# First-half v, k and q projections of a hybrid encoder layer at 512 columns, with their weights in borrowed rings

## The chip, the core and the metric

The kernel runs on one core of a Trainium2 chip. TensorE (PE) multiplies; its weight loads are shown as an engine of their own (PEld). VectorE (DVE), ScalarE (ACT) and GpSimd (POOL) do the rest, and SyncE (SP) issues every DMA of this kernel. The metric is the device time of one execution in microseconds, as a median of several executions.

## The reference

One layer of an encoder. Two inputs of width 1024, a prompt of 2048 tokens and a sample of 64 tokens, go through an RMS norm and one wide input projection; its columns feed a differential attention, a retention and their gates; two output projections, a merge and a last projection follow.

```python
def layer_inputs(x, norm_g, w_in, b_gate, qn_g, kn_g):
    h = rmsnorm(x, norm_g) @ w_in
    qa, ka, va, za, qb, kb, vb, zb, ga, gb = jnp.split(h, _split_points(), axis=-1)
    qa = rmsnorm(qa.reshape(B, T, H_A, 2, DK_A), qn_g)
    ka = rmsnorm(ka.reshape(B, T, H_A, 2, DK_A), kn_g)
    va = va.reshape(B, T, H_A, DV_A)
    ...

def layer_output(x, oa, ob, za, zb, ga, gb, subln_g, lam_init, w_oa, w_ob, w_out):
    oa = (rmsnorm(oa, subln_g) * (1.0 - lam_init)).reshape(B, T, W_A) * jax.nn.silu(za)
    ob = rmsnorm(ob).reshape(B, T, W_B) * jax.nn.silu(zb)
    m = ga * (oa @ w_oa) + gb * (ob @ w_ob)
    return x + m @ w_out
```

`qa`, `ka` and `va` (here q, k and v of the attention) have 512 columns each, four heads of 128. The normed k and v are outputs as well. Everything is float32.

## The kernel before

Every large product is made of three: both operands are split into a high part, rounded to the matmul's faster float32 form, and a low part, the difference; high x high, high x low and low x high are summed in PSUM.

The program is written by a planner in Python. Tasks are generators with priorities; a loop (line 80) runs the first task that is ready by estimated clocks of the engines (`P`, `A`, `V`, `G`, `ld`, lines 113 to 132), and what it emits fixes the order of instructions on TensorE, ACT and DVE. Buffers are rings counted by `take` and `give` (lines 97 to 111), with the sizes of `BUFS` (line 33). So each of these three engines runs its queue in a fixed order, and an instruction that waits holds all behind it.

The projections (`w_stream`, line 1442) go through the tokens in two halves of 1024; the sample belongs to the first. For each half they go through `w_in` in blocks of 256 columns.

- x: `x_prep` (line 247) loads tiles of 128 tokens, `x_norm` (272) norms them (sum of squares on ACT, line 277; small steps, lines 280 to 289; times the norm's weight `gn` on DVE, line 294). `gn` is a row of 1024 numbers, loaded into all 128 partitions by one DMA. `x_tile` (298) transposes a tile by TensorE (line 308, eight transposes) and splits it into `xh` and `xl` (lines 315, 316).
- W: `w_load` (332) loads a block of 256 columns in four pieces of 256 rows (two K blocks each, 256 KB) into the ring `ws` of 3; `w_split` (344) casts a piece to `wh` on ACT (line 354) and takes the difference `wl` on POOL (line 361; two of the first pieces on DVE, line 358) into the ring `w` of 12 tiles, which is six pieces.
- `mm_group` (374) issues the 24 products of one output: 8 K blocks x 3. `natural` (392) uses the x tile as weights and W as the moving operand, 256 columns wide; two x tiles share one PSUM bank and one evacuation. `transposed` (542) uses W as weights and moves up to 512 tokens.
- v is evacuated by `fin_va` (495), k and q by `fin_qk` (417; norm per head, four transposes, split, stores into DRAM scratch `kT`, `qT`). Their outputs pass through rings `ev` (3), `tlo` (2) and `thi` (1).

The first half's order is v (two blocks), k (two), q first block, mark `kqv0`, q second block, mark `kqv1`, then the retention's projections and the gates. `z_stream` (1497) starts the attention of heads 0 and 1 at `kqv0` of a half and that of heads 2 and 3 at `kqv1`; it loads k, v and q again from DRAM scratch through the rings `K` (4), `V` (4) and `q` (2), and `ath` and `atl` (2 each) hold split probabilities. Its tasks have a higher priority than projections, which fill TensorE otherwise. When both streams are done, the last stage makes the output projections (lines 1339 to 1341 and 1404 to 1406).

Ahead of everything stand 16 products of `ones` (line 1555) without use for the result.

## Time and profile before

| | us |
|---|---|
| median of 3 runs | 2037.01 (2036.58 to 2038.7) |
| the profiled execution | 2037.63 |
| its span, first to last instruction | 2035.9 |
| TensorE / ACT / DVE / POOL busy | 1999.1 / 962.7 / 985.9 / 420.5 |
| products at line 384, 256 columns, x as weights (3 groups) | 289, 283 and 283 ns each, 1024 in each group |
| products at line 384, 512 columns, W as weights (3 groups) | 397, 391 and 391 ns each, 768 in each group |

In the profile a line names the source line, the engine, the operation, the tile written and the tiles read, with shapes; the number in square brackets is how long the engine sat idle before it, and what ended that. The order "mm<-wh,xh" gives the moving operand first and the weights second. Products overlap: a product's own time is longer than the step from one start to the next, and the step is what counts for throughput. fp32 products, such as those of `ones`, stand as two records each.

### The profile page before, as it was taken

What the parts mean: (1) busy time and instruction counts of PE and PEld (TensorE: products, weight loads), DVE (VectorE), ACT (ScalarE), POOL (GpSimd) and SP (SyncE); (2) the same over time, 40 slices, a digit from 0 to 9 for tenths busy, and PEclk for the clock granted to TensorE, in tenths of its full rate; (3) what the DMA queues carried; (4) which work ended last, traced back from release to release, by engine and by line L of the source; (5) the groups of instructions that cost most, each with busy time, mean ns of one, the idle gap of its engine ahead of it and who ended that gap; (6) DMA issues with size and microseconds to landing.
All of it is one profiled execution on the core that took longest, in us unless ns stands there. A gap on an engine that the chain in (4) does not pass through costs nothing. (4 is left out here: it accounts for less than half of the span.)

```text
span 2035.9 us, 35819 instructions
## 1 busy us (share of the span) xinstructions
PE 1999.1 (98%) x13058; PEld 1826.1 (90%) x13058; DVE 985.9 (48%) x2671; ACT 962.7 (47%) x2123; POOL 420.5 (21%) x394
## 2 busy tenths in 40 slices
PE   7999999999999999999999999999999979999999
PEld 7999999999998999999999888888888868888997
DVE  6265765643331210546856545635653365444442
ACT  5334766644343332535766655634654453333321
POOL 1222112121012221221211212122131343222210
PEclk9999999999999999999999999999999989999999
DMA  6663545345565463563352252463233665454531
GB/s 217 202 195 115 162 138 145 101 124 156 151 170 133 130 194 93 152 200 127 113 155 91 84 154 75 115 188 99 63 100 113 187 200 154 144 150 136 148 101 58
DMA packets 332160, 281.57 MB, mean 138 GB/s; under 512 B 65104, under 2 KB 307408, under 8 KB 331984
## 3 DMA queue, kind: packets, MB, share of 16 engines
q1 hardware_dynamic: 331984, 279.29, 46.8%
q8 instruction: 103, 1.69, 0.4%
q14 instruction: 73, 0.60, 0.1%
HBM read 187.71 MB, written 91.49 MB: 137 GB/s over the span
## 5 line engine op out<-in xcount | busy, mean ns | idle before, releaser
L384 PE MATMUL mm<-xh,wh 128*128 128x512 f32 (+2 forms) x1280 | 459.8, 359 | 0.0
L384 PE MATMUL mm<-xh,wl 128*128 128x512 f32 (+2 forms) x1280 | 452.0, 353 | 0.0
L384 PE MATMUL mm<-xl,wh 128*128 128x512 f32 (+2 forms) x1280 | 451.7, 353 | 0.0
L361 POOL TENSOR_TENSOR wl<-ws,wh 128x512 fp32r<-128x512 f32 x190 | 252.1, 1342 | 832.5 <-ACT wh L354 643.5
L384 PE MATMUL mm<-wh,xh 128*128 128x256 f32 x1088 | 313.3, 288 | 0.5 <-ACT xh L315 0.3
L384 PE MATMUL mm<-wl,xh 128*128 128x256 f32 x1088 | 307.7, 283 | 0.7 <-DVE wl L358 0.3
L384 PE MATMUL mm<-wh,xl 128*128 128x256 f32 x1088 | 307.7, 283 | 0.2 <-DVE xl L316 0.2
L384 PEld LDWEIGHTS mm<-xh,wl 128*128 128x128 f32 x1280 | 241.0, 188 | 31.1
L384 PEld LDWEIGHTS mm<-xh,wh 128*128 128x128 f32 x1280 | 241.3, 189 | 30.6 <-issue 0.2
L384 PEld LDWEIGHTS mm<-xl,wh 128*128 128x128 f32 x1280 | 241.4, 189 | 30.0
L384 PEld LDWEIGHTS mm<-wh,xh 128*128 128x128 f32 x1088 | 204.8, 188 | 3.3 <-ACT xh L315 0.5
L384 PEld LDWEIGHTS mm<-wl,xh 128*128 128x128 f32 x1088 | 204.9, 188 | 3.0 <-DVE wl L358 0.5
L384 PEld LDWEIGHTS mm<-wh,xl 128*128 128x128 f32 x1088 | 204.7, 188 | 0.4 <-DVE xl L316 0.4
L569 ACT COPY ev<-mm 128x512 f32<-128x512 f32 x140 | 71.6, 512 | 213.4 <-PE mm L384 200.4
L865 DVE TENSOR_TENSOR atl<-at,ath 128x512 fp32r<-128x512 f32 (+1 forms) x144 | 93.6, 660 | 151.6 <-ACT ath L863 151.6
L782 ACT ACTIVATE row<-row,a_mx 128x1024 f32<-128x1024 f32 (+7 forms) x160 | 153.5, 963 | 24.2 <-DVE a_mx L762 24.0
L752 DVE CUSTOM_DVE_ANT_0 row<-s,dfar 128x512 f32<-128x512 f32 (+2 forms) x192 | 117.3, 631 | 72.4 <-PE s L744 71.3
L354 ACT CAST wh<-ws 128x512 fp32r<-128x512 f32 x192 | 117.0, 619 | 65.4 <-PE mm L384 37.5
L863 ACT CAST ath<-at 128x512 fp32r<-128x512 f32 (+1 forms) x144 | 79.6, 563 | 99.1 <-PE at L850 98.6
L743 PE MATMUL s<-K,q 128*128 128x512 f32 (+3 forms) x320 | 120.3, 381 | 3.0 <-DVE a_acc L752 2.8
L803 DVE SCALAR_TENSOR_TENSOR row<-row,a_w 128x1024 f32<-128x1024 f32 (+4 forms) x96 | 101.4, 1064 | 40.5 <-ACT row L800 40.2
L744 PE MATMUL s<-K,q 128*128 128x512 f32 (+3 forms) x320 | 115.7, 363 | 0.0
(196 smaller groups left out, 3922.1 us busy)
## 6 DMA issues: line engine op xcount, KB each, us to landing
ws<-in_w_in_dram SPq DMA_DIRECT2D x192, 256.0 KB, 3.0
q<-qT SPq DMA_DIRECT2D x128, 128.0 KB, 3.0
V<-vN SPq DMA_DIRECT2D x24, 512.0 KB, 5.4
K<-kT SPq DMA_DIRECT2D x48, 256.0 KB, 4.2
gt<-gaT SPq DMA_DIRECT2D x64, 132.0 KB, 2.1
gt<-gbT SPq DMA_DIRECT2D x64, 132.0 KB, 2.1
xt<-in_x_prompt_dram SPq DMA_DIRECT2D x16, 512.0 KB, 5.0
kn<-in_cache_k_T_dram SPq DMA_DIRECT2D x32, 256.0 KB, 3.2
```

The costliest lines, as they stand in the source:

```text
L354: nc.scalar.copy(h, st)
L361: nc.gpsimd.tensor_sub(l, st, h.bitcast(F32))
L384: nc.tensor.matmul(ps, p, q, start=c == 0 and i == 0, stop=c == KC - 1 and i == 2)
L569: nc.scalar.copy(ev, ps)
L743: nc.tensor.matmul(ps, q1s, kk, start=True, stop=False)
L744: nc.tensor.matmul(ps, q2s, kk, start=False, stop=True)
L752: nc.vector.tensor_tensor_reduce(out=units[k0 // 1024][:, k0 % 1024:k0 % 1024 + n], in0=ps, in1=tab, scale=-SLOPES[h], scalar=3.0e38, op0= ...
L782: nc.scalar.activation(u, u, AF.Exp, bias=mx, scale=-1.0, accum_out=lp[:, k:k + 1])
L803: nc.vector.scalar_tensor_tensor(out=u0, in0=u0, scalar=w[:, 0:1], in1=u1, op0=ALU.mult, op1=ALU.add)
L863: nc.scalar.copy(ah[:, :w], at[:, :w])
L865: nc.vector.tensor_sub(al[:, :w], at[:, :w], ah[:, :w].bitcast(F32))
```

## The change

In the first half v, k and q become one block of 512 columns each, in that order, and both marks come behind q. `natural` then takes one x tile to a PSUM bank (24 products of 512 columns, not 48 of 256). W comes in eight pieces of 128 rows x 512 columns for a block, each still 256 KB. Their split parts go into rings that are free at that time: v's and q's into the attention's `K` and `V` (as [128, 2, 512], two K blocks in a tile), k's first six K blocks into `w` and its last two into `q`. The first eight pieces are staged in `ws`, `ath` and `atl` together (`STAGE`). Odd pieces of these blocks have their difference on DVE. A W unit is now one K block throughout, and a ring's tile is given back when its last K block is used.

The weight row of the norm is loaded for the first half as a single row into a cleared tile `gz`; two products with `ones` (1/128 everywhere) spread it over the partitions, and DVE copies the result times 128 into `gn`. The warm-up has 12 products, not 16. The second x tile is loaded after four W pieces, the third after eight.

k, q and v are evacuated and stored one x tile at a time with all four heads (`nh=4`): `kT` and `qT` in runs of 128 tokens, `vN` and the outputs in rows of 512 columns. The second half is as before.

```diff
+STAGE = ["ws", "ws", "ws", "ath", "ath", "atl", "atl", "ws"]
...
-            yield lambda: self.xfly < XFLY and (half > 0 or self.wloads >= min(2 * j, 4))
+            yield lambda: self.xfly < XFLY and (half > 0 or self.wloads >= min(4 * j, 8))
...
-            if j == 0:
+            if j == 0 and half == 0:
+                tg = self.ld(self.gz[0:1, :], self.i["norm_g"][0:1, :], 4096)
+                self.ld(self.ident, self.i["c_ident"], 1 << 16)
+                for k in range(2):
+                    sl = slice(512 * k, 512 * k + 512)
+                    ps = self.psum("s")
+                    nc.tensor.matmul(ps, self.ones, self.gz[:, sl], start=True, stop=True)
+                    t = self.P(2048)
+                    nc.vector.tensor_scalar_mul(gn[:, sl], ps, 128.0)
+                    tg = self.V(512, t)
+                self.give("row", tg)
+            elif j == 0:
                 tg = self.ld(gn, self.i["norm_g"][0].partition_broadcast(128), 1 << 19)
-                if half == 0:
-                    self.ld(self.ident, self.i["c_ident"], 1 << 16)
...
-            for c0 in self.order[half]:
-                for q in range(4):
-                    yield from self.take("ws")
-                    st = self.sb(self.wp, [128, 2, 256], "ws")
+            for c0, wide in self.order[half]:
+                for q in range(8 if wide else 4):
+                    tag = STAGE[q] if self.wloads < 8 else "ws"
+                    yield from self.take(tag)
+                    pool = self.wp if tag == "ws" else self.ap
+                    if wide:
+                        st = self.sb(pool, [128, 512], tag, "ws")
+                        src = self.i["w_in"][0, 128 * q:128 * q + 128, c0:c0 + 512]
...
+    def w_room(self, wide, nw, q):
+
+        if not wide:
+            tags, pool, shape = ("w", "w"), self.wp, [128, 2, 256]
+        elif nw != 1:
+            tags, pool, shape = ("K", "V"), self.ap, [128, 2, 512]
+        elif q < 6:
+            tags, pool, shape = ("w", "w"), self.wp, [128, 1, 512]
+        else:
+            tags, pool, shape = ("q", "q"), self.ap, [128, 2, 512]
+        u = q % 2 if shape[1:] == [2, 512] else 0
+        if u == 0:
+            for tag in tags:
+                yield from self.take(tag)
+            self.wroom = [self.sb(pool, shape, tag, n, F32R) for tag, n in zip(tags, ("wh", "wl"))]
+        if not wide:
+            return self.wroom, tags
+        return [w[:, u] for w in self.wroom], tags if u == shape[1] - 1 else ()
...
-            if n in (0, 2):
-                yield t
-                nc.vector.tensor_sub(l, st, h.bitcast(F32))
-                t = self.V(512, t)
...
+                if wide and q % 2:
+                    yield t
+                    nc.vector.tensor_sub(l, st, h.bitcast(F32))
+                    t = self.V(512, t)
...
-    def natural(self, half, fin, fresh=False):
+    def natural(self, half, fin, fresh=False, wide=False):
         us = []
         tiles = self.xtiles(half)
-        for j0 in range(0, len(tiles), 2):
-            pair = tiles[j0:j0 + 2]
+        per, n = (1, 512) if wide else (2, 256)
+        for j0 in range(0, len(tiles), per):
+            group = tiles[j0:j0 + per]
...
-                self.give(tag, self.st(d[2 * g:2 * g + 2, :, t0:t0 + rt].rearrange("h p t -> p h t"),
-                                       s.bitcast(F32).rearrange("p (h t) -> p h t", h=2), nu << 17))
+                self.give(tag, self.st(d[hs, :, t0:t0 + rt].rearrange("h p t -> p h t"),
+                                       s.bitcast(F32).rearrange("p (h t) -> p h t", h=nh), nh * nu << 16))
...
-        first = ORD(fva0, fva, fk, fq, m0, m1)
+        wva = (va, lambda half: self.natural(half, self.fin_va(0, 4), True, True), True)
+        wk = (ka, lambda half: self.natural(half, self.fin_qk("k", 0, 4), False, True), True)
+        wq = (qa, lambda half: self.natural(half, self.fin_qk("q", 0, 4), False, True), True)
+        first = ([wva, wk, wq, m0, m1], ORD(fva0, fva, fk, fq, m0, m1))
...
+            self.res["row"].free.pop()
+            self.gz = self.row("gz")
+            nc.gpsimd.memset(self.gz, 0.0)
             warm = self.psum("at")
-            for _ in range(16):
+            for _ in range(12):
```

More of the change, by code (lines that the diff above doesn't have):

```diff
@@ L172, in consts @@
         self.ld(self.rzeta, i["c_rzeta"])
-        self.qinv = c("qinv", [128, 2, 8])
+        self.qinv = c("qinv", [128, 3, 8])
         for h in range(4):
@@ L177, in consts @@
                                  (SLOPES[h] / 0.125) ** 2 / 64.0)
+            nc.vector.memset(self.qinv[:, 2, 2 * h:2 * h + 2], (SLOPES[h] / 0.125) ** 2 / 64.0)
         self.gq = c("gq", [128, 1])
@@ L333, in w_load @@
         for half in range(2):
-            for c0 in self.order[half]:
-                for q in range(4):
-                    yield from self.take("ws")
-                    st = self.sb(self.wp, [128, 2, 256], "ws")
-                    t = self.ld(st, self.i["w_in"][0, 256 * q:256 * q + 256, c0:c0 + 256]
-                                .rearrange("(c p) n -> p c n", p=128), 1 << 18)
-                    self.wst.append((st, t))
+            for c0, wide in self.order[half]:
[7 more added lines that the diff above has]
+                    else:
+                        st = self.sb(pool, [128, 2, 256], tag)
+                        src = self.i["w_in"][0, 256 * q:256 * q + 256, c0:c0 + 256] \
+                            .rearrange("(c p) n -> p c n", p=128)
+                    t = self.ld(st, src, 1 << 18)
+                    self.wst.append((st, t, tag))
@@ L341, in w_load @@
                     self.wloads += 1
                     yield self.pe
+    def w_room(self, wide, nw, q):
[5 more added lines that the diff above has]
+            tags, pool, shape = ("w", "w"), self.wp, [128, 1, 512]
+        else:
+            tags, pool, shape = ("q", "q"), self.ap, [128, 2, 512]
[7 more added lines that the diff above has]
+        return [w[:, u] for w in self.wroom], tags if u == shape[1] - 1 else ()
@@ L344, in w_split @@
     def w_split(self):
         nc = self.nc
-        for n in range(4 * (len(self.order[0]) + len(self.order[1]))):
-            yield lambda: len(self.wst) > 0
-            st, t = self.wst.pop(0)
-            yield from self.take("w", 2)
-            if t > self.pe:
-                yield t
-            h = self.sb(self.wp, [128, 2, 256], "w", "wh", F32R)
-            l = self.sb(self.wp, [128, 2, 256], "w", "wl", F32R)
-            nc.scalar.copy(h, st)
-            t = self.A(512, self.pe)
-            if n in (0, 2):
-                yield t
-                nc.vector.tensor_sub(l, st, h.bitcast(F32))
-                t = self.V(512, t)
-            else:
-                nc.gpsimd.tensor_sub(l, st, h.bitcast(F32))
-                t = self.G(512, t)
-            self.give("ws", t)
-            self.wq.append((h, l, t))
+        nw = n = 0
@@ new lines, in w_split @@
+        for c0, wide in self.order[0] + self.order[1]:
+            for q in range(8 if wide else 4):
+                yield lambda: len(self.wst) > 0
+                st, t, tag = self.wst.pop(0)
+                (h, l), tags = yield from self.w_room(wide, nw, q)
+                if t > self.pe:
+                    yield t
+                nc.scalar.copy(h, st)
+                t = self.A(512, self.pe)
+                if wide and q % 2:
+                    yield t
+                    nc.vector.tensor_sub(l, st, h.bitcast(F32))
+                    t = self.V(512, t)
+                else:
+                    nc.gpsimd.tensor_sub(l, st, h.bitcast(F32))
+                    t = self.G(512, t)
+                self.give(tag, t)
+                if wide:
+                    self.wq.append((h, l, t, tags))
+                else:
+                    self.wq.append((h[:, 0], l[:, 0], t, ()))
+                    self.wq.append((h[:, 1], l[:, 1], t, tags))
+                n += 1
+            nw += wide
@@ L366, in w_unit @@
     def w_unit(self, us, c):
-        if len(us) <= c // 2:
+        if len(us) <= c:
             yield lambda: len(self.wq) > 0
             us.append(self.wq.pop(0))
-        u = us[c // 2]
+        u = us[c]
         if u[2] > self.pe:
             yield u[2]
-        return u[0][:, c % 2], u[1][:, c % 2]
+        return u
     def mm_group(self, ps, n, us, wsl, x, wfirst, last):
@@ L378, in mm_group @@
         for c in range(KC):
-            a, b = yield from self.w_unit(us, c)
+            a, b, _, tags = yield from self.w_unit(us, c)
             a, b = a[:, wsl], b[:, wsl]
@@ L385, in mm_group @@
                 self.P(n)
-            if c % 2:
-                if last:
-                    self.give("w", self.pe + LAT, 2)
-                if c < KC - 1:
-                    yield self.pe
-    def natural(self, half, fin, fresh=False):
+            if last:
+                for tag in tags:
+                    self.give(tag, self.pe + LAT)
+            if c % 2 and c < KC - 1:
+                yield self.pe
+    def natural(self, half, fin, fresh=False, wide=False):
         us = []
         tiles = self.xtiles(half)
-        for j0 in range(0, len(tiles), 2):
-            pair = tiles[j0:j0 + 2]
+        per, n = (1, 512) if wide else (2, 256)
+        for j0 in range(0, len(tiles), per):
+            group = tiles[j0:j0 + per]
             yield from self.take("mm")
             ps = self.psum("mm")
-            for u, (src, r, seg, col) in enumerate(pair):
+            for u, (src, r, seg, col) in enumerate(group):
                 if fresh:
@@ L402, in natural @@
                     yield self.xt_ready[j0 + u]
-                yield from self.mm_group(ps[:r, 256 * u:256 * u + 256], 256, us, slice(0, 256),
+                yield from self.mm_group(ps[:r, n * u:n * u + n], n, us, slice(0, n),
                                          (seg, slice(col, col + r)), False, j0 + u == len(tiles) - 1)
-                if u < len(pair) - 1:
+                if u < len(group) - 1:
                     yield self.pe
             t0 = 1024 * half + 128 * j0 if j0 < 8 else T
-            self.spawn(fin(ps[:r, :256 * len(pair)], r, len(pair), t0, self.pe + LAT), 0, "w")
+            self.spawn(fin(ps[:r, :n * len(group)], r, len(group), t0, self.pe + LAT), 0, "w")
             yield self.pe
@@ L415, in rows_out, with fin_qk @@
                        nu * nbytes)
-    def fin_qk(self, which, g):
+    def fin_qk(self, which, g, nh=2):
         nc = self.nc
         ep = self.ep
+        hs = slice(2 * g, 2 * g + nh)
         def fin(ps, r, nu, t0, t):
-            n, ng, rt = 256 * nu, 4 * nu, r * nu
+            n, ng, rt = 128 * nh * nu, 2 * nh * nu, r * nu
             yield from self.take("ev")
@@ L445, in fin @@
                 nc.vector.scalar_tensor_tensor(out=ms, in0=ms, scalar=64.0 * EPS,
-                                               in1=self.qinv[:r, g, :ng], op0=ALU.add, op1=ALU.mult)
+                                               in1=self.qinv[:r, 2 if nh == 4 else g, :ng], op0=ALU.add, op1=ALU.mult)
             else:
@@ L457, in fin @@
                 if t0 < T:
-                    dst = self.o["k_prompt"][0, 0, t0:t0 + rt, 2 * g:2 * g + 2]
+                    dst = self.o["k_prompt"][0, 0, t0:t0 + rt, hs]
                 else:
-                    dst = self.o["k_sample"][0, 0, :, 2 * g:2 * g + 2]
-                ts = self.rows_out(dst.rearrange("t h c d -> t (h c d)"), raw, nu, 1 << 17)
+                    dst = self.o["k_sample"][0, 0, :, hs]
+                ts = self.rows_out(dst.rearrange("t h c d -> t (h c d)"), raw, nu, nh << 16)
             yield from self.take("tp")
@@ L464, in fin @@
             for u in range(nu):
-                for h in range(2):
-                    nc.tensor.transpose(tp[:, h * rt + u * r:h * rt + u * r + r],
-                                        raw[:, u * 256 + h * 128:u * 256 + h * 128 + 128],
+                for h in range(nh):
+                    c = 128 * (nh * u + h)
+                    nc.tensor.transpose(tp[:, h * rt + u * r:h * rt + u * r + r], raw[:, c:c + 128],
                                         self.ident[:r, :r])
@@ L472, in fin @@
             yield from self.take("tlo")
-            hi = self.sb(ep, [128, 512], "thi", dt=F32R)[:, :2 * rt]
-            lo = self.sb(ep, [128, 512], "tlo", dt=F32R)[:, :2 * rt]
-            pt = tp[:, :2 * rt]
+            hi = self.sb(ep, [128, 512], "thi", dt=F32R)[:, :nh * rt]
+            lo = self.sb(ep, [128, 512], "tlo", dt=F32R)[:, :nh * rt]
+            pt = tp[:, :nh * rt]
             if which == "q":
@@ L490, in fin, with fin_va @@
                     yield w
-                self.give(tag, self.st(d[2 * g:2 * g + 2, :, t0:t0 + rt].rearrange("h p t -> p h t"),
-                                       s.bitcast(F32).rearrange("p (h t) -> p h t", h=2), nu << 17))
+                self.give(tag, self.st(d[hs, :, t0:t0 + rt].rearrange("h p t -> p h t"),
+                                       s.bitcast(F32).rearrange("p (h t) -> p h t", h=nh), nh * nu << 16))
         return fin
-    def fin_va(self, g):
+    def fin_va(self, g, nh=2):
         nc = self.nc
         ep = self.ep
+        hs = slice(2 * g, 2 * g + nh)
         def fin(ps, r, nu, t0, t):
-            n, rt = 256 * nu, r * nu
+            n, rt = 128 * nh * nu, r * nu
             yield from self.take("ev")
@@ L515, in fin @@
             if t0 < T:
-                dst = self.o["v_prompt"][0, 0, t0:t0 + rt, 2 * g:2 * g + 2]
+                dst = self.o["v_prompt"][0, 0, t0:t0 + rt, hs]
             else:
-                dst = self.o["v_sample"][0, 0, :, 2 * g:2 * g + 2]
+                dst = self.o["v_sample"][0, 0, :, hs]
             yield t1
-            gsl = slice(256 * g, 256 * g + 256)
-            self.give("thi", self.rows_out(self.vN[0][t0:t0 + rt, gsl], hi.bitcast(F32), nu, 1 << 17))
+            gsl = slice(256 * g, 256 * g + 128 * nh)
+            self.give("thi", self.rows_out(self.vN[0][t0:t0 + rt, gsl], hi.bitcast(F32), nu, nh << 16))
             yield t2
-            td = self.rows_out(dst.rearrange("t h e -> t (h e)"), raw, nu, 1 << 17)
+            td = self.rows_out(dst.rearrange("t h e -> t (h e)"), raw, nu, nh << 16)
             if t0 == T:
@@ L527, in fin @@
             yield t3
-            self.give("tlo", self.rows_out(self.vN[1][t0:t0 + rt, gsl], lo.bitcast(F32), nu, 1 << 17))
+            self.give("tlo", self.rows_out(self.vN[1][t0:t0 + rt, gsl], lo.bitcast(F32), nu, nh << 16))
         return fin
@@ L1466, in w_stream @@
         seqs = [f + seq for f in first]
-        self.order = [[c for c, _ in q if c is not None] for q in seqs]
+        self.order = [[(c[0], len(c) > 2) for c in q if c[0] is not None] for q in seqs]
         self.seg_free = [0.0, 0.0]
@@ L1476, in w_stream @@
         for half in range(2):
-            for k, (c0, f) in enumerate(seqs[half]):
+            for k, (c0, f, *_) in enumerate(seqs[half]):
                 if c0 is None:
@@ L1572, in ORD @@
 def ORD(va0, va, k, q, m0, m1):
-    return ([va0, va[1], k[0], k[1], q[0], m0, q[1], m1],
-            [va0, k[0], q[0], m0, va[1], k[1], q[1], m1])
+    return [va0, k[0], q[0], m0, va[1], k[1], q[1], m1]
 def const_arrays():
```

## The prediction

> **What bounds the kernel now.** The page first: the share of each engine in the span.

> ```profile
> span 2035.9 us, 35819 instructions
> PE 1999.1 (98%) x13058; PEld 1826.1 (90%) x13058; DVE 985.9 (48%) x2671; ACT 962.7 (47%) x2123; POOL 420.5 (21%) x394
> ```

> TensorE is in use for 98% of the span and no other engine for half of it. So time is won in two ways only: the same products in less TensorE time, or fewer of TensorE's pauses. To see where the pauses are I read the table of stretches (PE, weight loads, DVE, ACT, POOL busy, then granted clock, DMA share, GB/s), by 5 us at the start and around the change of stage at the end.

> ```profile
> 15.00:20.00 5.00, 4.67 (x39) 4.41 (x38) 3.29 (x9) 4.91 (x13) 1.10 (x1) 1.00 1.02 372
> 20.00:25.00 5.00, 0.88 (x8) 0.64 (x6) 2.10 (x5) 4.94 (x13) 1.93 (x2) 0.82 0.57 148
> 25.00:30.00 5.00, 4.04 (x19) 4.04 (x20) 4.79 (x12) 4.69 (x12) 1.44 (x1) 0.50 0.64 202
> 50.00:55.00 5.00, 5.00 (x45) 5.00 (x44) 0.69 (x1) 2.83 (x6) 1.43 (x2) 1.00 0.33 108
> ```

> From 20 to 25 us TensorE does 8 transposes in 5 us, at 25 to 30 its clock is half, and ACT is full. From 50 on it runs without a gap. The pause in the order of time on TensorE:

> ```profile
> 20.28 0.60 PE L308 MATMUL pv<-ident,xt 128*128 128x128 f32 x4
> 25.96 1.12 PE L308 MATMUL tp<-ident,xt 128*128 128x128 f32 x4 [5.09 <-DVE xl L316]
> ```

> The transposes of the fourth x tile stand in TensorE's queue ahead of ready products and wait for DVE, which waited on ACT (3 us in one piece, in the row of DVE's wait for the `raw` copy below). The granted clock of 0.82 and then 0.50 in the two stretches above makes 0.36 x 5 + 5 = 6.8 us at half speed.

> ```profile
> 22.79 0.69 DVE L512 TENSOR_TENSOR tlo<-mm,thi 128x512 fp32r<-128x512 f32 x1 [3.00 <-ACT raw L510]
> ```

> **The width.** Steps from start to start, TensorE in the order of time: in the K stage (nine products between the two rows), in a transposed group (24 products of 512 between the two), in the last output tile (64-row weights, 512 wide, six between), and the sample tile of the first V block (24 between).

> ```profile
> 89.08 0.28 PE L384 MATMUL mm<-wh,xl 128*128 128x256 f32 x1
> 90.16 0.28 PE L384 MATMUL mm<-wh,xl 128*128 128x256 f32 x1
> ```

> ```profile
> 765.79 0.39 PE L384 MATMUL mm<-xh,wh 128*128 128x512 f32 x1
> 771.26 0.28 PE L384 MATMUL mm<-xh,wh 128*128 128x256 f32 x1
> ```

> ```profile
> 2021.24 0.40 PE L1404 MATMUL at<-woh,ms 128*64 128x512 f32 x1
> 2022.63 0.40 PE L1404 MATMUL at<-woh,ms 128*64 128x512 f32 x1
> ```

> ```profile
> 51.70 0.28 PE L384 MATMUL mm<-wh,xh 128*64 128x256 f32 x1
> 54.44 0.28 PE L384 MATMUL mm<-wh,xh 128*128 128x256 f32 x1
> ```

> That is 1.08/9 = 0.120 us at 256 wide, 5.47/24 = 0.228 at 512, 1.39/6 = 0.232 at 512 with 64 rows, 2.74/24 = 0.114 at 256 with 64 rows. A full x tile costs 48 x 0.120 = 5.76 us for 512 columns before, 24 x 0.228 = 5.47 after: 0.29 less. There are 8 full tiles and 3 projections: 24 x 0.29 = 7.0 us. The sample tile costs 24 x 0.232 = 5.57 against 2 x 2.74 = 5.48, three times 0.09: 0.3 more. **Steady gain 6.7 us.** Upper bound: the 512-wide step at its narrowest inside that group is 0.227 (which gives 24 x 0.31 = 7.5); lower bound: 0.232 everywhere, 24 x 0.19 = 4.6. I take 6.7, since the 24-product row has the same full 128-row weights. The transposes of K and Q are as many as before (four for each full evacuation), as are the evacuations' lengths (512 columns).

> [...]

> **The start.** Rows of TensorE, ACT and DVE of the first microseconds:

> ```profile
> 1.05 6.26 PE L1555 MATMUL at<-ones 128*128 128x128 f32 x32 [1.05 <-DVE epst L1552]
> 6.04 0.15 DVE L284 TENSOR_SCALAR x_st<-x_st 128x1 f32<-128x1 f32 x1 [5.04 <-ACT xjk L277]
> 6.61 0.22 DVE L287 SCALAR_TENSOR_TENSOR x_st<-x_st 128x1 f32<-128x1 f32 x1 [0.41 <-ACT x_st L281]
> 7.24 1.28 DVE L294 SCALAR_TENSOR_TENSOR xt<-xt,x_st,gn 128x1024 f32<-128x1024 f32 x1
> 8.58 0.66 PE L308 MATMUL tp<-ident,xt 128*128 128x128 f32 x4 [1.27 <-DVE xt L294]
> 9.07 0.60 PE L308 MATMUL pv<-ident,xt 128*128 128x128 f32 x4
> ```

> and ACT's groups of the first 50 us (busy in all, mean ns):

> ```profile
> L277 ACT ACTIVATE xjk<-xt 128x1024 f32<-128x1024 f32 (+1 forms) x9 | 9.5, 1052 | 2.9 <-DMA xt<-in_x_prompt_dram 2.9
> L315 ACT CAST xh<-pv 128x512 fp32r<-128x512 f32 (+1 forms) x9 | 5.1, 563 | 1.6 <-PE pv L308 1.5
> L354 ACT CAST wh<-ws 128x512 fp32r<-128x512 f32 x6 | 3.7, 622 | 3.3 <-DMA ws<-in_w_in_dram 3.3
> ```

> Before: the first V block ends at 54.44. Its work is 8 x 24 x 0.120 = 23.0 for full tiles, 2.7 for the sample tile, and transposes of nine x tiles, 8 x 2 x 0.49 + 0.8 = 8.6 (0.49 from the rows at 8.58 and 9.07; the half tile taken as one half): 34.3. So 20.1 us of the first 54.4 do no work. After, step by step:

> 1. Warm-up. 12 instead of 16 matmuls, each two records; 6.26/16 = 0.39, so the end is at about 5.8 instead of 7.3.
> 2. The weight row. SP waits for POOL's clearing of `gz` ahead of the loads of the identity and of W behind it. No row clears so much; its bounds are the 0.2 us of four constants and two 512-wide POOL operations at 1.27 (2.5). I take 1.3, between, as it reads nothing: SP goes on at about 1.7 to 2.9. The load of one row lands in the 2.2 us of `gq`, by 4 to 5.5, under the warm-up; W lands while the x chain below runs. Cost on the path: 0, and up to 1.5 if the x tile were not the later one.
> 3. Two fp32 products of 512 columns. The nearest row is line 611, two records for 256 columns, 0.59 in all with 0.378 for one, so a record each 0.21: 4 x 0.21 = 0.86 for 512, 1.7 for both. From 5.8: 6.9 and 7.8 with the latency.

> ```profile
> L611 PE MATMUL tp<-r_sq,ones x66: 377/378/383, 219.9 to 1540.7; 128*128 128x256 f32 x66
> 607.27 0.59 PE L611 MATMUL tp<-r_sq,ones 128*128 128x256 f32 x2
> 9.49 1.27 POOL L361 TENSOR_TENSOR wl<-ws,wh 128x512 fp32r<-128x512 f32 x1 [9.05 <-ACT wh L354]
> gq<-in_qn_g_dram SPq DMA_DIRECT2D x2, 0.2 KB, 2.2
> gn<-in_norm_g_dram SPq DMA_DIRECT2D x1, 512.0 KB, 5.4
> ```

> 4. DVE copies both halves (0.69 each, as line 512) ahead of the first x tile's chain in its queue: the second ends near 8.6. Then lines 284 to 289, 0.8 (from 6.04 to 7.24, less the wait of 0.41 for ACT), and line 294, 1.28: the first transposes start near 10.8, **2.2 later than 8.58**. This is what the exchange of a 512 KB load for a row costs; it gives back DMA time, 5.4 us to landing, for W and x behind it.
> 5. Behind the first transposes the third product waits for ACT's cast and DVE's difference of the first half tile, 0.56 + 0.69, of which the second set of transposes covers 0.49: 0.8 us idle, today as well as after.
> 6. Then each x tile brings 5.47 us of products instead of 2.9. ACT owes a tile 1.05 + 2 x 0.56 = 2.2 us for the sum of squares and the split, two copies of an evacuation at 0.6 each, and on top small operations and W's casts (0.62). Today an evacuation serves two tiles: 2.8 and the rest against 2.9 + 0.98 = 3.9 us of TensorE, and x tiles come in bunches; so ACT is full and TensorE waits. After, 3.4 and the rest stand against 5.47 + 0.98 = 6.4. So the 5.09 us pause loses its cause, and the half clock with it. What is late next: W blocks 4 to 7, whose casts share ACT with the second x tile. I put 1 us there and 1 for transposes of later tiles queued too early: 2.

> Idle after: 10.8 + 0.8 + 2 = 13.6, against 20.1: **gain 6.5 us.** Bounds: with no later wait 8.5; with today's pause and half clock again (5.1 and half of 6.8 us in place of the 2) 20.1, nothing.

> **Stores, order, rings.** K and Q tiles are now stored 128 tokens at a time, in runs of 512 B instead of 1 KB. Rows from the loads and stores (us to landing last):

> ```profile
> kT<-thi SPq DMA_DIRECT2D x16, 256.0 KB, 2.5
> obT<-rru SPq DMA_DIRECT2D x64, 64.0 KB, 1.7
> V<-vN SPq DMA_DIRECT2D x24, 512.0 KB, 5.4
> V<-vN SPq DMA_DIRECT2D x4, 512.0 KB, 7.1
> ```

> `obT` and `vN` are 512 B runs already. A quarter of the size lands in 1.7, twice the size in 5.4, so about 3 for 256 KB, 0.5 more than today; the single `thi` buffer is then held 0.56 + 3 = 3.6 of the 5.9 us between tiles (5.47 and a set of four transposes): hidden. Cost 0; the upper end is a rival.

> The mark that lets heads 0 and 1 begin moves behind the whole of Q.

> ```profile
> 192.07 0.28 PE L384 MATMUL mm<-wh,xl 128*64 128x256 f32 x1
> 194.34 0.22 PE L743 MATMUL s<-K,q 128*128 128x128 f32 x1
> 808.75 0.15 DVE L284 TENSOR_SCALAR x_st<-x_st 128x1 f32<-128x1 f32 x1 [64.86 <-ACT xjk L277]
> 1600.00:1641.00 41.00, 37.89 (x174) 31.12 (x172) 17.01 (x29) 19.33 (x48) 16.31 (x20) 1.00 0.63 190
> ```

> Today attention starts (194.34) just as the second Q block ends, one block (8 x 2.88 + 2.74 and its transposes, about 28 us) after its mark. After, the mark comes at 192 - 13 = 179 and attention at about 207, 13 later. It is covered: DVE sits idle for 64.86 us up to 808.75, when the first half's attention and retention are over and projections alone fill TensorE. Those now run earlier in exchange. K and V rings are lent to W until Q is done; head loads (5.4 to 7.1 us for V) fit into the 28. Both halves still load W in the same number of 256 KB pieces, and casts and differences are as many. Cost 0.

> **Sum.** 2037.63 (the profiled execution; its span is 1.7 less, and that lies outside) - 6.7 - 6.5 = 2024.4. The profiled execution stands 0.6 above the median, so 2023.8; I say **2024**. Its own range: 2037 - 7.5 - 8.5 = 2021 to 2037 - 4.6 - 3 = 2029.

> **Rivals.**

> *The start is not better* (0.14). The gap between row products and transposes (7.6 to 10.8) is 3 us, and today a gap of 5 brought half clock; with that, and transposes again queued too early, 20 us idle. For it: ACT is full from 15 to 30 today. Against: step 6. Time: 2037 - 6.7 = 2030. [...]

> *One `thi` buffer* (0.08), the slower side. If a 256 KB store of 512 B runs lands in L, the buffer is held 0.56 + L, and each of 16 full K and Q tiles waits 0.56 + L - 5.9 once L is over 5.3; at 6.2 it has eaten the 13 us. At the 7.1 of four V loads in a crowded stretch: 16 x 1.8 = 28, so 2052. For it: twice as many runs for the same bytes. Against: these stores land in 2.5 today.

> *The later attention comes out at the end* (0.07). If the last stage waited for attention, 13 us come back: 2037, within 0.2%. For it: TensorE has gaps in 1600 to 1641. Against: the 65 us of cover, and the second half's order is untouched.

> *The 512-wide step is set by the weight load* (0.01), 0.192 us as the mean of the natural groups' loads, and not by the columns: 576 x (0.240 - 0.192) = 28 us, 2037 - 28 - 6 = 2003. Three rows above say 0.227 to 0.232.

> ```profile
> L384 PEld LDWEIGHTS mm<-wh,xh 128*128 128x128 f32 x1024 | 196.1, 192 | 3.3 <-ACT xh L315 0.5 <-PE s L744 0.4
> ```

> That the change doesn't do what it says would show as 256-wide products in the first 190 us; nothing in the diff lets that happen.

> **Numbers.** Forecast 0.70. About 0.2% (4 us) is what a measurement of this kernel can tell from no change. Faster: 0.70 + 0.14 + 0.01 = 0.85; same 0.07; slower 0.08. The range 2018 to 2031 holds the forecast with a reserve of 3 us below its own range for what shifts at the change of stage, and the first rival.

> **What would show it.** TensorE with about 12,400 products; 512-wide steps of 0.227 to 0.228 under `mm<-wh,xh`; first transposes near 10.8 and no pause over 2 us after it; granted clock 1.00 from 10 to 50; first V projection ended near 14 + 57 = 71 us; the last Q product near 179; first attention product near 207, and DVE's idle stretch before the second half's norm shorter than 65 us. I'm wrong if the start's idle time is still 20, if ACT waits at `thi` for stores, or if attention's delay shows in a longer gap after the last projection.

## The result and the profile after

The changed kernel takes **2029.43 us** (median of 6 runs, 2028.33 to 2030.77) against 2036.96 (2036.38 to 2038.7) for the kernel before on the same chip: ratio 0.9962, 95% interval 0.9949 to 0.9975, so 7.5 us or 0.4% faster. The forecast was 2024. On another chip, in the last of the runs below, it was 2028.25 against 2037.30, 0.9954 (0.9940 to 0.9968). The profiled execution shown here took 2029.37 us, span 2027.6.

The share of the engines, from the page after:

```profile
span 2027.6 us, 34426 instructions
...
PE 1991.4 (98%) x12406; PEld 1787.8 (88%) x12406; DVE 1003.2 (49%) x2671; ACT 956.3 (47%) x2112; POOL 410.5 (20%) x385
```

TensorE is in use for 98% of the span as before, with 652 records fewer: 648 products from the width (1296 of 256 columns became 648 of 512) and 8 of the shorter warm-up, less 4 that the spread adds. The places in TensorE's order of time that separate the stages (first K product, first product of the block behind Q, first attention product), of the kernel after:

```profile
78.56 0.40 PE L427 MATMUL mm<-wh,xh 128*128 128x512 f32 x1
79.94 0.40 PE L427 MATMUL mm<-wh,xh 128*128 128x512 f32 x1
185.64 0.39 PE L427 MATMUL mm<-wh,xl 128*64 128x512 f32 x1
185.87 0.28 PE L427 MATMUL mm<-wh,xh 128*128 128x256 f32 x1
213.99 0.22 PE L789 MATMUL s<-K,q 128*128 128x128 f32 x1
```

and the first K product of the kernel before, when both of its V blocks are done:

```profile
80.20 0.28 PE L384 MATMUL mm<-wh,xh 128*128 128x256 f32 x1
```

and the first product of the last stage, of the kernel before and of the kernel after:

```profile
1634.36 0.28 PE L1339 MATMUL mm<-ogh,w_o_diffh 128*128 128x264 f32 x1
1625.78 0.29 PE L1385 MATMUL mm<-ogh,w_o_diffh 128*128 128x264 f32 x1
```

K and Q took 185.87 - 78.56 = 107.3 us; before, from 80.20 to the row at 192.07 and its step of 0.11, they took 112.0. So **4.7 us came from K and Q**, and only **1.6 from everything up to the end of V** (80.20 to 78.56), of which V's own products should have given over 2. The start itself gained nothing. The remaining 2 us of the span's 8.3 came between 186 us and the last stage; I did not follow them.

What the start looks like now, in the table of stretches after (PE, weight loads, DVE, ACT, POOL busy, granted clock, DMA share, GB/s):

```profile
5.00:10.00 5.00, 2.09 (x8) 0.78 (x6) 3.36 (x6) 2.47 (x7) 2.53 (x2) 1.00 0.91 325
10.00:15.00 5.00, 3.63 (x12) 3.01 (x13) 3.87 (x5) 2.83 (x6) 0.00 (x0) 0.58 1.04 401
15.00:20.00 5.00, 4.62 (x15) 3.31 (x13) 3.99 (x6) 3.51 (x9) 2.81 (x2) 0.74 0.96 378
25.00:30.00 5.00, 4.26 (x23) 3.38 (x21) 4.69 (x11) 4.90 (x15) 2.08 (x1) 1.00 0.54 184
30.00:35.00 5.00, 3.71 (x14) 3.31 (x15) 4.52 (x11) 4.50 (x12) 1.27 (x1) 0.66 0.82 240
```

The clock column is the news. 0.58 and 0.74 are (0.42 + 0.26) x 5 / 0.5 = 6.8 us at half speed right behind the first transposes, and 0.66 is another 3.4 us. This is one execution: in a second profile of the same kernel ("after, beside" below) 3.4 us at half speed follow the first transposes and none come later. TensorE's own rows, after:

```profile
5.20 1.88 PE L271 MATMUL s<-gz,ones 128*128 128x512 f32 x4
11.37 1.12 PE L319 MATMUL tp<-ident,xt 128*128 128x128 f32 x4 [4.28 <-DVE xt L305]
12.28 1.06 PE L319 MATMUL pv<-ident,xt 128*128 128x128 f32 x4
13.16 0.79 PE L427 MATMUL mm<-wh,xh 128*128 128x512 f32 x1
28.66 0.60 PE L319 MATMUL pv<-ident,xt 128*128 128x128 f32 x4
31.29 1.11 PE L319 MATMUL tp<-ident,xt 128*128 128x128 f32 x4 [2.03 <-DVE xl L327]
```

The spread ends at 7.08, then TensorE waits 4.28 us for the first x tile; four transposes take 1.12 us there and 0.60 at full speed. At 31.29 stands a wait that the prediction had dropped: the fourth x tile's transposes, queued directly behind the third's, ahead of products that were ready. DVE's and POOL's rows, which set the 11.37:

```profile
6.26 0.69 DVE L273 TENSOR_SCALAR gn<-s 128x512 f32<-128x512 f32 x1 [5.26 <-PE s L271]
7.12 0.69 DVE L273 TENSOR_SCALAR gn<-s 128x512 f32<-128x512 f32 x1 [0.17 <-PE s L271]
7.73 0.14 DVE L295 TENSOR_SCALAR x_st<-x_st 128x1 f32<-128x1 f32 x1
8.01 0.53 DVE L298 SCALAR_TENSOR_TENSOR x_st<-x_st 128x1 f32<-128x1 f32 x1
8.76 1.23 DVE L300 TENSOR_TENSOR x_st<-x_st 128x1 f32<-128x1 f32 x1
10.03 1.28 DVE L305 SCALAR_TENSOR_TENSOR xt<-xt,x_st,gn 128x1024 f32<-128x1024 f32 x1
```

```profile
0.73 0.95 POOL L1604 MEMSET gz<- 128x1024 f32 x1 [0.29 <-POOLq L1666]
7.25 1.27 POOL L398 TENSOR_TENSOR wl<-ws,wh 128x512 fp32r<-128x512 f32 x1 [5.57 <-ACT wh L391]
8.71 1.26 POOL L398 TENSOR_TENSOR wl<-ws,wh 128x512 fp32r<-128x512 f32 x1 [0.19 <-ACT wh L391]
```

Read the two together: DVE's one-column operation at 8.01 ends at 8.54, when POOL's first difference ends (8.52); the one at 8.76 ends at 9.99, with POOL's second (9.97).

### The profile page after: what moved, and what is told of

Read it like the earlier page. It is cut to its first block, busy times and chain, and to the rows that moved or that the text cites. A ratio compares the mean times of both kernels' runs of the same rounds, so it can differ in the third digit from the quotient of the medians.

```text
span 2027.6 us, 34426 instructions
## 1 busy us (share of the span) xinstructions
PE 1991.4 (98%) x12406; PEld 1787.8 (88%) x12406; DVE 1003.2 (49%) x2671; ACT 956.3 (47%) x2112; POOL 410.5 (20%) x385
## 5 line engine op out<-in xcount | busy, mean ns | idle before, releaser
L398 POOL TENSOR_TENSOR wl<-ws,wh 128x512 fp32r<-128x512 f32 x180 | 239.3, 1339 | 926.8 <-ACT wh L391 602.5
L427 PE MATMUL mm<-wh,xh 128*128 128x256 f32 (+3 forms) x872 | 276.6, 317 | 0.3 <-DVE tlo L558 0.3
L427 PE MATMUL mm<-wh,xl 128*128 128x256 f32 (+3 forms) x872 | 271.0, 311 | 0.0
L427 PE MATMUL mm<-wl,xh 128*128 128x256 f32 (+3 forms) x872 | 270.8, 311 | 0.0
L427 PEld LDWEIGHTS mm<-wh,xh 128*128 128x128 f32 (+1 forms) x872 | 164.6, 189 | 11.7 <-PE s L790 0.4
L427 PEld LDWEIGHTS mm<-wl,xh 128*128 128x128 f32 (+1 forms) x872 | 164.8, 189 | 11.1
L427 PEld LDWEIGHTS mm<-wh,xl 128*128 128x128 f32 (+1 forms) x872 | 164.3, 188 | 10.9 <-DVE xl L327 0.2
## 6 DMA issues: line engine op xcount, KB each, us to landing
ws<-in_w_in_dram SPq DMA_DIRECT2D x192, 256.0 KB, 3.0
V<-vN SPq DMA_DIRECT2D x24, 512.0 KB, 5.4
K<-kT SPq DMA_DIRECT2D x48, 256.0 KB, 4.2
xt<-in_x_prompt_dram SPq DMA_DIRECT2D x16, 512.0 KB, 6.3
kn<-in_cache_k_T_dram SPq DMA_DIRECT2D x32, 256.0 KB, 3.9
```

The lines of the kernel that those rows point to most:

```text
L398: nc.gpsimd.tensor_sub(l, st, h.bitcast(F32))
L427: nc.tensor.matmul(ps, p, q, start=c == 0 and i == 0, stop=c == KC - 1 and i == 2)
```

## The experiments

Theory A: the spread of the weight row is what the start lost by. It holds the first transposes, and the pause in front of them halves the clock. Rival B: W's arrival and splitting bound the start anyway, so the way of the row does not matter. All times are medians of 5 or more runs (but for one profile alone). Four chips served: one for kernels 1 to 4, one for 5 to 7, one for 8 and the filler again, one for the three "beside". On them the kernel before took 2036.9, 2035.7, 2038.8 and 2037.3 us, so the ratios are what to compare. "K at" is the first product behind V, the end of the start; "output at" the first product of the last stage; "half" the time at half clock before 50 us, counted from the first change of the clock that the trace records. These columns come from the one profiled execution. Where a kernel has two profiles, they differ by up to 1.1 us in "K at" and "output at" and by up to 6.8 us in "half".

| kernel | us | ratio (95%) | first transposes | K at | output at | half |
|---|---|---|---|---|---|---|
| before | 2036.96 |  | 8.58 | 80.20 | 1634.4 | 6.8 |
| after | 2029.43 | 0.9962 (0.9949 to 0.9975) | 11.37 | 78.56 | 1625.8 | 10.2 |
| 1 row by DMA | 2026.05 | 0.9949 (0.9936 to 0.9961) | 8.43 | 75.36 | 1621.9 | 6.8 |
| 2 spread alone | 2039.14 | 1.0010 (1.0001 to 1.0018) | 12.33 | 81.92 | 1636.3 | 6.8 |
| 3 filler | 2028.27 | 0.9963 (0.9951 to 0.9975) | 11.54 | 75.42 | 1621.5 | 0 |
| 3 filler, again | 2025.63 | one run | 11.56 | 76.25 | 1622.6 | 3.4 |
| 4 differences on DVE | 2029.23 | 0.9965 (0.9953 to 0.9978) | 10.58 | 76.89 | 1625.2 | 3.4 |
| 5 tiles one ahead | 2024.64 | 0.9949 (0.9936 to 0.9961) | 11.05 | 74.99 | 1621.1 | 3.4 |
| 6 = 1 + 5 | 2025.11 | 0.9944 (0.9932 to 0.9957) | 7.89 | 73.81 | 1618.9 | 0 |
| 7 = 1 + 4 + 5, 22 warm-ups | 2023.68 | 0.9943 (0.9930 to 0.9957) | 8.09 | 72.85 | 1620.2 | 0 |
| 8 = 3 + 4 + 5 | 2027.15 | 0.9951 (0.9937 to 0.9964) | 11.38 | 74.57 | 1622.1 | 0 |
| after, beside 5 and 7 | 2028.25 | 0.9954 (0.9940 to 0.9968) | 11.73 | 77.46 | 1624.7 | 3.4 |
| 5, beside | 2028.27 | 0.9949 (0.9936 to 0.9961) | 11.93 | 75.88 | 1621.5 | 3.4 |
| 7, beside | 2025.79 | 0.9935 (0.9923 to 0.9948) | 8.71 | 72.86 | 1619.7 | 0 |

No edit touches what comes behind "output at", yet the 14 profiles need between 400.3 and 403.8 us for it. Their granted clock is half for 10.2 to 17.1 us between 1631 and 1679 us, where the last stage begins: the five profiles with 10.2 us take 400.3 to 401.8, the three with 17.1 take 402.6 to 403.3, the six between them 400.9 to 403.8. So a difference of 2 or 3 us between two medians can come from there, and "output at" shows a change of the start with less of it.

**1 and 2: each half of the change alone.** The first has the width, W's order and the rings, with the row loaded as before; the second is the kernel before with those lines of the change's diff that spread the row, and 12 warm-ups.

```diff
 kernel 1, against the kernel after
-            if j == 0 and half == 0:
-                tg = self.ld(self.gz[0:1, :], self.i["norm_g"][0:1, :], 4096)
...
-            elif j == 0:
+            if j == 0:
                 tg = self.ld(gn, self.i["norm_g"][0].partition_broadcast(128), 1 << 19)
+                if half == 0:
+                    self.ld(self.ident, self.i["c_ident"], 1 << 16)
...
-            for _ in range(12):
+            for _ in range(16):
```

> The kernel after, but the norm weight comes by the old 512 KB broadcast load and 16 warm-up products stand ahead again; widths, rings and staging stay. Theory A (the spread is what costs the start: DVE's two copies hold the first x tile's chain until 11.4 us and the gap on TensorE from 6.9 to 11.4 brings half clock): first transposes back near 8.6 to 9.5, no half clock before 20 us, time 2023 to 2026. Rival B (the start is bound by x and W arriving and by ACT, whatever the weight row does; the 512 KB load pushes W back by 1 to 2 us): products of the first tile wait for W, time 2029 to 2032.

> The kernel before with nothing of the change but the weight row spread by TensorE and 12 warm-up products; all projections 256 wide. Theory A: first transposes near 10.5 to 11.4, so 1 to 4 us slower than before, 2038 to 2041. Rival B (512 KB less to load lets x and W arrive earlier): same or up to 2 us faster, 2035 to 2037.

Kernel 1, TensorE in the order of time:

```profile
8.43 0.66 PE L310 MATMUL tp<-ident,xt 128*128 128x128 f32 x4 [1.20 <-DVE xt L296]
12.77 0.77 PE L418 MATMUL mm<-wl,xh 128*128 128x512 f32 x1 [1.45 <-DVE wl L386]
75.36 0.40 PE L418 MATMUL mm<-wh,xh 128*128 128x512 f32 x1
```

Kernel 2, the same view:

```profile
6.21 1.88 PE L269 MATMUL s<-gz,ones 128*128 128x512 f32 x4
12.33 0.66 PE L317 MATMUL tp<-ident,xt 128*128 128x128 f32 x4 [4.23 <-DVE xt L303]
```

All of the change but the spread (width, order of loads, rings) is worth 10.9 us (2036.9 to 2026.05); the spread alone costs 2.2 and its interval lies just above 1. Together that is 8.7 faster, near the 7.5 and 9.1 of the two measurements of the whole change. Theory A holds for the row: 2026.05 stands at the upper end of what it expected. Rival B has a part: with the x tile early, TensorE waits 1.45 us for a low part of W, and half a clock comes at 12.8 all the same, which theory A had not expected. In kernel 2 the first transposes came 0.9 us later than the 11.4 expected; there a difference of W, 1.64 us beside one on POOL, stands in DVE's queue ahead of the x tile's steps.

**3: the pause filled.** Idle products behind the spread, into a bank that nobody reads.

```diff
                 self.give("row", tg)
+                for _ in range(18):
+                    nc.tensor.matmul(self.warm[:, 0:128], self.ones, self.ones, start=True, stop=True)
...
-            warm = self.psum("at")
+            warm = self.warm = self.psum("at")
```

> The kernel after with 18 idle products of ones (3.9 us at full clock) on TensorE between the two spreading products and the first transposes; every other queue as it is. Theory A (the gap makes the clock fall at about 10.8 for 6.8 us, which costs half of that): granted clock 1.00 to 20 us, the first V block ends 3 to 4 us earlier, time 2025 to 2027. Rival B (W pieces and the second x tile set the end of the first tile, so faster products wait for them): clock 1.00 but the same end, 2029.

> The kernel with 18 idle products after the spread once more, for a second profile, since its timed runs lay from 2023.8 to 2034.4 us. If the spread of its times comes from the clock in the start, a time above 2027 us goes with at least 3.4 us of half clock before 50 us, and a time near 2024 us with none. If the start is at full clock and the time is above 2027 us, the difference lies elsewhere in the span.

TensorE's rows of the first of the two profiles:

```profile
7.53 4.18 PE L276 MATMUL at<-ones 128*128 128x128 f32 x36
11.54 0.60 PE L321 MATMUL tp<-ident,xt 128*128 128x128 f32 x4
19.75 0.63 PE L321 MATMUL tp<-ident,xt 128*128 128x128 f32 x4 [2.07 <-DVE xt L307]
30.59 0.66 PE L321 MATMUL tp<-ident,xt 128*128 128x128 f32 x4 [2.03 <-DVE xl L329]
```

and the stretches of the second:

```profile
10.00:15.00 5.00, 4.62 (x29) 3.55 (x28) 4.11 (x7) 3.02 (x7) 0.21 (x2) 1.00 1.04 406
30.00:35.00 5.00, 4.34 (x16) 3.41 (x17) 4.89 (x8) 4.93 (x12) 1.28 (x1) 0.69 0.67 204
```

The transposes start 0.2 us later than after, take 0.60 in place of 1.12, and K begins 3.1 us sooner in the first profile, 2.3 in the second (2.0 and 1.2 against the kernel after's second profile). In both the half clock behind the first transposes is gone; both profiles of the kernel after have it, and those of kernels 2, 4 and 5. The order of every engine's other instructions is the same as after, so the pause brings it. Rival B has a part here too: the second x tile's transposes now wait 2.07 us, at 19.75, in place of 0.82. The last stage begins at 1621.5 and 1622.6, against 1625.8 and 1624.7 after. The timed gain stays open (ratios 0.9963 and 0.9962): the runs went from 2023.8 to 2034.4. They follow the mean granted clock of the execution:

```
us     2023.76  2026.54  2027.63  2028.91  2029.18  2034.36
clock    0.997    0.997    0.996    0.995    0.995    0.994
```

0.001 of the clock is 2 us of this span, so some 6 of the 10.6 us are half clock somewhere; only the execution of 2023.76 us has a profile, so where the longer ones had it is not shown. The second profile answers neither branch of its expectation, 2025.63 us with 3.4 us of half clock, but it shows one cause: the same wait of 2.03 us (ended at 30.59 in the one, at 30.66 in the other) stayed without effect in one execution and halved the clock in the other.

**4: POOL away from DVE.** The first eight pieces of W get both differences on DVE; the queues of TensorE and ACT are as after.

```diff
-                    nc.gpsimd.tensor_sub(l, st, h.bitcast(F32))
+                    (nc.vector if n < 8 else nc.gpsimd).tensor_sub(l, st, h.bitcast(F32))
```

> The kernel after with the differences of the first eight W pieces all on DVE (four of them move from POOL), at the same places of the order; TensorE's and ACT's queues are the same. Theory A (DVE's small two-operand instructions of the first x tile are held while POOL works on a W piece: 0.53 and 1.23 us in place of 0.2 and 0.16): they take 0.2 us again, first transposes near 10.6 for 11.4, time lower by 0.5 to 2. Rival B (the two are late for another reason, and DVE gets 2.8 us of work more): they stay long, time the same or 1 to 2 higher.

DVE, and TensorE's first transposes, of kernel 4:

```profile
8.60 0.22 DVE L298 SCALAR_TENSOR_TENSOR x_st<-x_st 128x1 f32<-128x1 f32 x1
9.04 0.16 DVE L300 TENSOR_TENSOR x_st<-x_st 128x1 f32<-128x1 f32 x1
9.23 1.28 DVE L305 SCALAR_TENSOR_TENSOR xt<-xt,x_st,gn 128x1024 f32<-128x1024 f32 x1
```

```profile
10.58 0.97 PE L319 MATMUL tp<-ident,xt 128*128 128x128 f32 x4 [3.49 <-DVE xt L305]
```

0.53 and 1.23 us are 0.22 and 0.16 again, so POOL's concurrent operation was what held them. A difference of 0.68 now stands in their place, and the transposes come 0.8 sooner. In the time it is nothing that can be told: 2029.23, where 0.5 to 2 less was expected.

**5 to 7: the order of tiles, and all together.** In 5 a tile from the fourth on is transposed in the middle of the product before its own, and its norm queues behind the copies of the tile before it.

```diff
-        yield t2
+        yield t2; yield lambda: j < 3 or self.vdone > 72 or len(self.xt_ready) >= j
...
-        yield lambda: len(self.xq) > j and self.xq[j] is not None
+        yield lambda: len(self.xq) > j and self.xq[j] is not None and (j < 3 or self.vdone >= 8 * j - 4)
...
-            a, b = a[:, wsl], b[:, wsl]
+            a, b, self.vdone = a[:, wsl], b[:, wsl], self.vdone + 1
```

Kernel 6 is the same on kernel 1, and 7 adds to 6 the edit of 4 and

```diff
-            for _ in range(16):
+            for _ in range(22):
```

> The changed kernel, spread kept, with one difference: in the first half a token tile from the fourth on is transposed in the middle of the V product of the tile before it, not back to back with it, and its norm is queued on VectorE behind the copy of the tile before. Theory C (the wait of 2.2 us at 29 us and the half clock after it come from the order of TensorE's queue): the wait goes, the window of half clock at 31 to 35 us may go with it, the last V product ends 2 to 4 us sooner (75 to 76.5 us in place of 78.6) and the time is 2025.5 to 2027.5 us. Rival D (the tile's norm is held by VectorE and the loads, so the same idle time comes out at a later tile): the last V product ends within 1 us of 78.6 and the time stays 2028.5 to 2030.

> The norm weight row by its old DMA (as in the run with the row by DMA, 2026.05 us) and the tiles one ahead as in the run sent with this one. Theory C: 2 to 4 us less than with the row by DMA alone, 2022 to 2024 us, the wait of 2.8 us at 26 us gone. Rival D: 2025.5 to 2026.5 us. If the two edits are independent, the difference to the other run of this pair is the 3.4 us that the row by DMA was worth by itself.

> The run before it with two more differences: the first eight pieces of W have both their differences on VectorE, and 22 warm-up products in place of 16, which end near the first transposes at 8.4 us. Theory: the wait of 1.6 us for a piece's low part at 10.9 us and the half clock at 12.8 us go, together 1.6 to 3.2 us: 2019 to 2022 us. Rival: VectorE's own queue (eight differences of 0.69 us ahead of the second tile's norm) delays the second tile by as much as was won: 2022 to 2024.5 us.

In the second profile of kernel 5 the wait is shorter and no longer in front of ready products, and the clock stays full behind it (as it did, in that pair, behind the 2.03 us of the kernel after):

```profile
28.39 0.60 PE L319 MATMUL pv<-ident,xt 128*128 128x128 f32 x4
30.30 0.50 PE L427 MATMUL mm<-wh,xh 128*128 128x512 f32 x1 [1.30 <-ACT xh L326]
```

K begins 1.6 to 3.6 us sooner (75.88 and 74.99 against 77.46 and 78.56). On the first chip the time, 2024.64, went 0.9 us below theory C's range; beside the kernel after on the last chip it did not follow:

> The changed kernel itself, on one chip with the two below, since the kernel before has differed by up to 3 us from chip to chip. By its first times 7.5 us under the kernel before (ratio 0.9962). Its profile is also a second look at the start: if the pause of 4.5 us before the first transposes is what brings half the clock, windows of half clock lie between 10 and 18 us again.

> Tiles one ahead, spread kept. Theory C: 2.5 to 5 us under the changed kernel on the same chip, with the last V product 2 to 4 us sooner. Rival: within 1.5 us of it, the first difference having come from the chip.

> Row by DMA, tiles one ahead, the first eight differences of W on VectorE, 22 warm-ups. 4 to 7 us under the changed kernel on the same chip; rival: no better than the run above, since only one of its edits counts in the end (within 1 us of it).

2028.27 against 2028.25: by the medians the order alone is worth nothing that these runs can tell, by its ratios (0.9949 twice, against 0.9962 and 0.9954) 1 to 3 us. In the profiles the last stage begins 3.2 us sooner beside it (1621.5 against 1624.7) and 4.7 sooner on the first chip, so up to there the order gains; how much of it the whole time keeps stays open. Kernel 6, expected at 2022 to 2024, missed with 2025.11, 0.9 under kernel 1 on another chip. Kernel 7 has the lowest median on both of its chips. Its ratio is 0.0019 below that of the kernel after each time, 4 us, but the intervals overlap, and kernel 6 (0.9944) can't be told from it. It lies 11.5 to 12.0 us below the kernel before; beside the kernel after the medians differ by 2.5, less than the 4 to 7 expected. Its first run, 2023.68, fell into the rival's 2022 to 2024.5 and not the theory's 2019 to 2022, although the wait for a low part went from 1.46 us (kernel 6) to 0.46; the half clock that it was to remove was absent from kernel 6's profile already. Its stretches in the second profile, with no half clock:

```profile
5.00:10.00 5.00, 4.76 (x37) 4.52 (x35) 2.60 (x7) 3.25 (x8) 0.00 (x0) 1.00 0.98 332
10.00:15.00 5.00, 4.55 (x17) 3.13 (x18) 4.89 (x9) 4.45 (x10) 0.00 (x0) 1.00 1.04 403
25.00:30.00 5.00, 3.12 (x15) 2.11 (x14) 2.73 (x3) 4.91 (x14) 2.00 (x2) 1.00 0.44 118
```

**8: the same with the spread.** Kernel 5 with the edits of 3 and 4, so that against 7 almost only the row's way differs:

```diff
-                for _ in range(18):
+                for _ in range(16):
```

> The changed kernel, spread kept, with tiles one ahead, the first eight differences of W on VectorE and 16 idle products on TensorE between the spread and the first transposes. Against the run of all three edits with the row by DMA (2023.68 us) only the row's way differs. Theory A (the spread holds the first transposes about 2.5 us longer than the DMA, 10.6 against 8.1 us, and nothing makes it up): 2025 to 2027 us in the timed runs and a last V product 2 to 3 us later than 72.9 us. Rival E (the start waits for W and the second tile in any case, so the row's way no longer matters): 2023 to 2024.5 us, last V product within 1 us of 72.9.

K at 74.57 against 72.85: the row's way still costs 1.7 us in the profile, between the theory's 2 to 3 and the rival's 1, and the last stage begins 1.8 to 2.4 us later (1622.1 against 1620.2 and 1619.7). 2027.15 lies just above the theory's 2025 to 2027, on a chip where the kernel before took 2038.8, and the ratios, 0.9951 and 0.9943, can't part the two.

## Why the prediction was right in one half and wrong in the other

**Right: the width.** The step at 512 columns is 0.230 us in K (six from 78.56 to 79.94), 0.228 forecast. K and Q by themselves should have given 16 x 0.29 - 0.2 = 4.4 us and gave 4.7. With this step the rival of 0.192 us is out.

**Wrong: the start, 6.5 us forecast and none measured.** With the work as the prediction counts it (8 x 5.47 + 5.57 + 8.6 = 57.9), 78.56 leaves 20.7 us idle in place of 13.6; before it was 20.1. Step by step:

- Steps 1 to 3 held: `gz` cleared in 0.95 us (1.3), spread done at 7.08, and at 7.98 in the second profile (7.8). The 0.39 us for a warm-up product is a mean over two clocks, which the section on the hardware explains; an early change to full clock, not the estimate, made the 7.08.
- Step 4 had the right chain, and put its end at 10.8, but two of its one-column operations took 1.4 us longer than alone (0.53 and 1.23 for 0.22 and 0.16), as experiment 4 undid. That is why it was 11.37 although the copies came 0.8 sooner than forecast.
- Steps 4 and 6 failed together in one point: a pause was charged for its own length only. Step 6 let the half clock go with the pause of 5.09 us, while step 4 made a new one of 3 us, in the event 4.28, in front of the first transposes. It halved the clock for 6.8 us in this execution and 3.4 in the second profile, which costs half of that; experiment 3 shows that the pause is the cause.
- Step 6's 2 us for all that comes later was too small: 0.82 at 20.44, then 2.03 at 31.29, here with 3.4 us of half clock behind it. It was right that the 5.09 goes. The cause it named, ACT, is only a part: the fourth tile's transposes stood ahead of products that were ready.
- Step 5's 0.8 us were not seen: no wait at half speed, and 0.24 us in kernel 5, where the clock was still full.

So what came is the first rival, with its price (2030) and its mechanism: a gap between the row's products and the transposes, half clock, transposes queued too early, 20 us idle, which the prediction had named as a sign of being wrong. It had 0.14 where the forecast had 0.70. That 2029.43 lies between 2018 and 2031 is owed to the room that the range left for this rival, not to the forecast's working: the sum's own range ended at 2029. That end was also too low by its own terms, since it counted 3 us for the start, whose lower bound was nothing; 2037 - 4.6 would be 2032. The start that the forecast described exists: 72.85 of kernel 7 leaves 15.0 us idle. But it needs the row by DMA and two more edits.

**The other points.** Stores of 512 B runs land in 2.6 us (about 3 estimated), so the `thi` rival fell. From the last Q product to the first attention product there are 28.35 us (28 forecast); both came 7 us late, at 185.6 and 214.0, which is about what the start lacked. The later attention stayed covered, by DVE's shorter idle stretch ahead of the second half's norm:

```profile
795.64 0.15 DVE L295 TENSOR_SCALAR x_st<-x_st 128x1 f32<-128x1 f32 x1 [50.95 <-ACT xjk L288]
```

The 2 us between 186 and 1626 stood in none of its terms and were luck: without them the sum would have been off by more.

## What to carry to other kernels

Price a pause of TensorE twice: its length, and the half clock that can follow. The pause ahead of the first transposes (4.28 us in the first profile of the kernel after) was followed by 6.8 us at half clock there and by 3.4 in the second profile; of the 66 windows of 3.4 us that were less than half busy (table below), 55 had the next one at half clock. Idle products that reached up to the first real ones took the second price away in the three profiles that had them; the timed medians did not show the gain. A load that looks expensive (512 KB here) was the cheaper way beside the warm-up, 2026.05 us with it and 2029.43 with the spread in its place, which puts two copies of 0.69 us on DVE ahead of the first tile's steps; measure each half of a change alone before keeping both.

## What the runs showed of the hardware

```
busy share      windows   next at half clock
below 0.38           40                   40
0.38 to 0.50         26                   15
0.50 to 0.65         44                    1
0.65 and above     8037                    0
```

At half clock, all 10 windows below 0.8 busy kept it and all 53 above 0.9 ended it. Most windows ahead of a half clock were not idle as a whole: 37 of the 40 below 0.38 were busy for at least 0.1 of their time. The filler's two profiles agree with the table: the wait of 2.03 us left its window busy for 1.93 of 3.41 us (0.57) in the one, where the clock stayed full, and for 1.38 (0.40) in the other, where it halved. So a pause of 2.03 us was enough in one of the two.

TensorE ran at half speed in the first microseconds too, although the tables show 1.00 there: the records of the warm-up follow each other every 0.21 us up to the first entry that the trace has for the clock (3.95 us after, 6.16 before), and every 0.11 us after it. That entry came at 3.95 to 7.00 us in the 14 profiles, so 12 warm-up products ended at 5.37 us in one execution (after) and at 6.54 in another (5, beside), and part of the differences in "first transposes" is this phase.

**DVE was held to the end of a POOL operation.** A one-column DVE operation on two tensors took 1.25 us beside POOL's difference of W (at 17.35, after) in place of 0.16 to 0.22, and ended within 0.02 us of it. The one at 7.73 above, which reads one tensor, took its usual 0.14 beside POOL's difference at 7.25 (1.27 us).
